# Recurrent branch's last part in 22 steps of one weight tile each, and more tiles between block transposes and their readers

## The chip, the cores and the metric

The kernel runs on one core of one Trainium2 chip. The metric is the device time of one execution in microseconds (us); the median of several runs is compared. The engines are TensorE (PE, matmuls; PEld is its weight load), VectorE (DVE), ScalarE (ACT), GpSimd (POOL) and SyncE (SP, which here only issues DMAs).

## The reference

One decoder layer on 256 tokens of width 2048, all in float32. `rmsnorm(x)` is multiplied by one wide matrix `w_in`, whose columns feed three branches and three merge gates:

- A: attention with 8 heads of 128 over a block of 256 tokens (there is only one block, so it is plain causal attention), times `silu(gate)`.
- B: attention with 16 query heads of 64, 4 key heads, a window of 128 and sinks, times `silu(gate)`.
- C: a convolution of 4 taps, then a gated linear recurrence, times `silu(gate)`:

```python
r = sigmoid(conv_block @ w_r + b_r);  i = sigmoid(conv_block @ w_i + b_i)
log_a = -8 * r * softplus(-lam);      a = exp(log_a)
b = sqrt(max(-expm1(2 * log_a), 0)) * (i * conv)
h[t] = a[t] * h[t-1] + b[t]
```

Each branch's output of width 1024 is projected to 2048, weighted by its sigmoid merge gate and summed; the sum goes through `w_out` and is added to x. A gated per-layer embedding and a last norm follow.

## The kernel before

**Weights.** Every weight matrix streams through in tiles of 128 x 1024 float32 (512 KB). `fetch` issues the load on SP into one of four raw buffers. `split` (lines 118, 119) makes two parts of it: ACT casts it to the high part `wh`, DVE subtracts and gives the low part `wl`; each has four buffers. `mm3` (lines 162 to 164) multiplies high by high, low by high, and high by low. A tile has 12 matmuls of 512 columns. A raw buffer is free again when DVE has made the low part.

**Order.** The tile framework's planner simulates the engines and writes each engine's order. Instructions come by their place in the program; `split` is moved ahead by a priority offset (LEAD), so casts and low parts run some three tiles ahead of PE. `issue_after(x)` ties an instruction behind `x` on the same engine. `tick()` is called once for each weight tile, right behind its `split`. It runs timers that are due (`later(SETTLE, ...)`) and takes one step from the list `todo`, all tied behind the newest cast on ACT and the newest low part on DVE. `hand_out` puts the steps of several generators into `todo`: a new one begins every `period` ticks (11 in branch A, 7 in B), and every step advances all that live.

**Exchange through DRAM.** `flip` (lines 582 to 587) turns a matrix: a block transpose on DVE, a DMA of the tile to DRAM, and four DMAs back, all issued on SP. Readers take `flipped` views. For a SiLU gate, `silu` flips the projected half and registers `gate` (lines 455, 456) SETTLE ticks later. For attention probabilities, `turned_probs` flips and then yields LATE times before `split_probs` (lines 611, 612) reads; `py`, the product with the values, follows. A pair of heads goes through these steps: bias (and, for each second pair of B, the group's key and value splits), scores (`q_b`, lines 688, 689), maximum (552 to 559), exponential (566), AHEAD ticks later norm (571 to 575) and flip, LATE ticks later `w_b` and `py`, and in the last step the final part (708 to 712 and the split of `zb`).

**Branch C.** `branch_c` is a generator. It projects and convolves, does the block products `pg`, and yields. The gate's SiLU and tanh, exponential and square over all 2048 columns come after the query projection of branch A, the bound, square root and the scaled inputs after the key projection, and the scans, the gated result and its split after the first gate half. These parts are not tied to ticks.

**Stages on the path.** In order: norm and value projections, branch C's and branch A's projections, merge of C (48 weight tiles, in which A's attention steps run), branch B's projections, merge of A (in which most of B's steps run), merge of B, `w_out`, and the embedding part.

Of the kernel before, what the change touches and what calls it, by code (L numbers as in the profile page):

```python
# [38 lines left out]
SLOT = 2112  # L39
QD = 32  # L40
AHEAD = 4
STEPS = 14
LATE = 5
TURN_LATE = 5
SETTLE = 8
RV = 384


# [1 line left out]
def trunk(ctx: ExitStack, tc: tile.TileContext, x, xt, p, table, onehot, maskv, w_in, sinks, conv, w_ri, vec, fin, w_br,  # L50
# [17 lines left out]
    def cols(k, n=1):  # L68
        return slice(k * SEQ, (k + n) * SEQ)
# [23 lines left out]
    los = []  # L93
    todo = []
    timers = []
    loads = []
    first_parts = {}

# [26 lines left out]
    def tick():  # L125
        due = []
        for t in timers:
            t[0] -= 1
            if t[0] == 0:
                due.append(t)  # L130
        timers[:] = [t for t in timers if t[0] > 0]
        if due or todo:
            with tc.issue_after(casts[-1]), tc.issue_after(los[-1]):
                for t in due:
                    t[1]()
                if todo:
                    todo.pop(0)()

    def drain():
        while todo:  # L140
            tick()
# [78 lines left out]
    def act_of(*units):  # L220
        return [tuple(t[:, cols(k)] for t in u) for u in units for k in range(KB)]

    def as_tiles(t):
        return t.rearrange("p (m a q) -> p m a q", a=4, q=QD)

    def split_act(u, k, n, src):
        hi, lo = (x[:, cols(k, n)] if len(src.shape) == 2 else as_tiles(x[:, cols(k, n)]) for x in u)
        ins = nc.scalar.copy(hi, src).ins
        nc.vector.tensor_tensor(lo, src, hi.bitcast(F32), op=ALU.subtract)
        return ins  # L230
# [209 lines left out]
    def chunk(t, c):  # L440
        return t[:, c * NH * CW : (c + 1) * NH * CW]

    def features(t, scale, name):
        for c in range(2):
            to_features(chunk(t, c), in_chunk(), scale, f"{name}{c}")
# [14 lines left out]
    def branch_c():  # L460
        xcT, cv, wri = block("xcT"), block("cv"), block("wri")
        rg, ig = block("rg"), block("ig")
        W1 = SEQ + CONV - 1
        xp = xcT[:, : KB * W1].rearrange("p (k t) -> p k t", k=KB)
        nc.vector.memset(xp[:, :, : CONV - 1], 0.0)
        cvk, rk, ik, hk = ktiles(cv), ktiles(rg), ktiles(ig), ktiles(xcT)
        wr = wri[:, : 2 * BW].rearrange("p (n d) -> p n d", n=KB)
        for c in range(2):
            t = temp(f"xc{c}").rearrange("p k t -> p (k t)")
            to_features(t, in_chunk(), rs1, f"xc{c}")  # L470

            def place(c=c, t=t):
                for h in range(NH):
                    to = xp[:, 4 * c : 4 * c + 4, CONV - 1 + h * P : CONV - 1 + (h + 1) * P]
                    nc.scalar.copy(to.rearrange("p j (a q) -> p j a q", a=4), flipped(t, 8)[:, h::NH])

            later(SETTLE, place)
        with tc.issue_after(casts[-1]):
            nc.scalar.dma_start(wri[:, : 2 * BW], w_ri)
        z = unit("zc")  # L480
        gs = [temp(f"gc{c}").rearrange("p k t -> p (k t)") for c in range(2)]
        for c in range(2):
            to_features(gs[c], in_chunk(), rs1, f"gc{c}")
        for k in range(KB):
            nc.vector.tensor_scalar(cvk[:, k, :], xp[:, k, 0:SEQ], convw[:, k : k + 1], conv_b[:, k : k + 1],
                                    op0=ALU.mult, op1=ALU.add)
            for j in range(1, CONV):
                nc.vector.scalar_tensor_tensor(cvk[:, k, :], xp[:, k, j : j + SEQ],
                                               convw[:, j * KB + k : j * KB + k + 1], cvk[:, k, :],
                                               op0=ALU.mult, op1=ALU.add)  # L490
            pg = aux(f"pg{k}")
            xs = split_small(cvk[:, k, :], f"cv{k}")
            ws = split_small(wr[:, k, :], f"wr{k}")
            for g in range(2):
                mm3(pg[:, g * SEQ : (g + 1) * SEQ], [t[:, g * P : (g + 1) * P] for t in ws], xs, True, True)
                nc.scalar.activation((rk, ik)[g][:, k, :], pg[:, g * SEQ : (g + 1) * SEQ], AF.Sigmoid,
                                     bias=(b_r, b_i)[g][:, k : k + 1])
            nc.vector.tensor_scalar_mul(rk[:, k, :], rk[:, k, :], sp8[:, k : k + 1])
            nc.vector.tensor_tensor(ik[:, k, :], ik[:, k, :], cvk[:, k, :], op=ALU.mult)
        yield  # L500
        for c in range(2):
            s = temp(f"sig_gc{c}").rearrange("p k t -> p (k t)")
            nc.scalar.activation(s, gs[c], AF.Sigmoid)
            nc.vector.tensor_tensor(gs[c], gs[c], s, op=ALU.mult)
        n = KB * SEQ
        t, a, sq, i = xcT[:, :n], rg[:, :n], cv[:, :n], ig[:, :n]
        nc.scalar.activation(t, a, AF.Tanh)
        nc.scalar.activation(a, a, AF.Exp, scale=-1.0)
        nc.scalar.activation(sq, a, AF.Square)
        yield  # L510
        nc.vector.scalar_tensor_tensor(sq, sq, 1.0, t, op0=ALU.add, op1=ALU.mult)
        nc.vector.tensor_scalar_max(sq, sq, 0.0)
        nc.scalar.activation(sq, sq, AF.Sqrt)
        for c in range(4):
            o = cols(2 * c, 2)
            nc.vector.tensor_tensor(i[:, o], i[:, o], sq[:, o], op=ALU.mult)
        yield
        for c in range(2):
            o = cols(4 * c, 4)
            for k in range(4 * c, 4 * c + 4):  # L520
                nc.vector.tensor_tensor_scan(hk[:, k, :], rk[:, k, :], ik[:, k, :], 0.0, op0=ALU.mult, op1=ALU.add)
            g = flipped(gs[c], 8)
            nc.vector.tensor_tensor(g, g, as_tiles(xcT[:, o]), op=ALU.mult)
            split_act(z, 4 * c, 4, g)
        yield z

    quad = [slice(i * QD, (i + 1) * QD) for i in range(P // QD)]

# [60 lines left out]
    def flipped(t, n):  # L589
        return t.rearrange("p (a m q) -> p m a q", a=4, m=n)  # L590
# [136 lines left out]
    for c in range(2):  # L727
        token_values(vh, (first_ps, second_ps)[c], c * CW)

    def branch_a(between):  # L730
        qT, kT, g = block("qa"), block("ka"), block("ga")
        features(qT, rs_q[DA], "qa")
        between()
        features(kT, rs1, "ka")
        between()
        silu(chunk(g, 0), "ga0")
        between()
        silu(chunk(g, 1), "ga1")
        va = [[vh[:, c, h * DA : (h + 1) * DA] for h in range(NA)] for c in range(NH)]
        return attention_heads(feature_tiles(qT), feature_tiles(kT), va, g)  # L740

    def branch_b():
        qT, kv, g = block("qb"), block("kvb"), block("gb")
        ps = in_chunk()
        kT = kv[:, : 2 * SEQ]
        vt = ktiles(kv)[:, 2:4, :]
        to_features(kT, ps[:, :, : 2 * P], rs1, "kb")
        token_values(vt, ps[:, :, 2 * P :], 0)
        features(qT, rs_q[DB], "qb")
        kb = [flipped(kT, 4)[:, NH * i : NH * (i + 1)] for i in range(2)]  # L750
        todo.extend([lambda: None] * 3)
        z = attention_pairs(feature_tiles(qT), kb, vt, g)
        for c in range(2):
            silu(chunk(g, c), f"gb{c}")
        return z
# [41 lines left out]
    def merge(z, bi, br):  # L797
        if bi == 0:
            merged.extend(wide(block(f"merged{h}")) for h in range(2))
        for n in range(4):  # L800
            sg = token_major(temp(f"sg_{br}{n}"))
            ps = in_chunk()
            for h in range(NH):
                nc.scalar.activation(sg[:, h, :], ps[:, h, :], AF.Sigmoid, scale=rs1[:, h : h + 1])
            if bi == 2 and n == 0:
                drain()
            py = project(act_of(z), w_br, (bi * 4 + n) * KB * CW // WT, f"br{br}{n}")
            dst = merged[n // 2][:, :, half_cols(n)]
            if bi == 0:
                nc.vector.tensor_tensor(dst, py, sg, op=ALU.mult)  # L810
                continue
            nc.vector.tensor_tensor(sg, py, sg, op=ALU.mult)
            (nc.vector if bi == 2 else nc.gpsimd).tensor_tensor(dst, dst, sg, op=ALU.add)
            if bi == 2:
                if n % 2 == 0:
                    mT.append(unit(f"m{n // 2}"))
                (turn_later if n < 3 else turn)(mT[n // 2], n, merged[n // 2], "m")

    steps = branch_c()
    next(steps)  # L820
    zcs = []
    za = branch_a(lambda: zcs.append(next(steps)))
    zc = zcs[-1]
    merge(zc, 0, "c")
    drain()
    zb = branch_b()
# [154 lines left out]
```

## Time and profile before

| | us |
|---|---|
| median of 3 runs | 1006.89 |
| lowest, highest | 1005.89, 1007.75 |
| the profiled execution | 1007.54 |
| its span | 1005.8 |
| PE busy in it | 984.7 (98%) |
| DVE busy | 658.2 (65%) |
| ACT busy | 555.5 (55%) |

The span is what the profiler's records cover; the execution's own time is 1.7 us longer. The shares are means over stages. The granted clock of TensorE was full (1.00, 2.4 GHz) in all slices between the first and the last.

### The profile page before, as it was taken

How to read it: one execution, taken by the hardware profiler on the slowest of the kernel's cores; microseconds unless marked ns; L12 is line 12 of the kernel's file. 1: busy time of each engine (PE TensorE's matmuls, PEld its weight loads, DVE VectorE, ACT ScalarE, POOL GpSimd, SP SyncE). 2: the span in 40 equal slices, each digit the busy share in tenths (PEclk: the TensorE clock that was granted, in tenths of full speed). 3: DMA queues.
4: the chain of work that ended last, by engine and by line, in shares of the span. 5: the costliest groups of instructions: out<-in, count | busy, mean ns of one | idle time of the engine just before them, and what ended most of it. 6: DMA issues, size and time to landing. Idle time of an engine off the chain costs nothing.

```text
span 1005.8 us, 12594 instructions
## 1 busy us (share of the span) xinstructions
PE 984.7 (98%) x4510; PEld 819.1 (81%) x4510; DVE 658.2 (65%) x950; ACT 555.5 (55%) x780; POOL 16.5 (2%) x14
## 2 busy tenths in 40 slices
PE   9999999999999999999999889999999999999996
PEld 7888888888788888888888768878888888888886
DVE  5765766665966567554577778796556655665764
ACT  7644446558565656544457557755444444554652
POOL 0000000000000000000000011011000000000000
PEclk9999999999999999999999999999999999999998
DMA  9867777665786665657777857677577776779652
GB/s 325 310 192 241 252 241 241 226 233 177 241 282 229 243 198 191 216 191 229 256 241 230 236 183 240 208 219 238 199 230 231 239 275 210 247 252 321 222 189 84
DMA packets 82774, 231.59 MB, mean 230 GB/s; under 512 B 9320, under 2 KB 30232, under 8 KB 82200
## 3 DMA queue, kind: packets, MB, share of 16 engines
q1 hardware_dynamic: 76176, 218.14, 66.5%
q10 hardware_dynamic: 6536, 12.65, 3.5%
q8 instruction: 35, 0.57, 0.2%
q14 instruction: 27, 0.22, 0.1%
HBM read 210.53 MB, written 20.22 MB: 229 GB/s over the span
## 4 chain that ended last, share of the span: by engine, by line
PE 80%; DVE 7%; DMA 5%; ACT 4%; issue 3%; SPq 1%; ACTq 0%; POOLq 0%; POOL 0%; DVEq 0%
PE ps_in L163 17%; PE ps_in L164 17%; PE ps_in L162 17%; PE ps_out L162 3%; PE ps_out L164 3%; PE ps_out L163 3%; PE ps_pg L162 3%; PE ps_pg L163 3%; PE ps_pg L164 3%; DVE wl_in L119 2%; PE ps_brc L162 1%; PE ps_brc L164 1%; PE ps_brb L164 1%; PE ps_brb L162 1%; PE ps_brc L163 1%
## 5 line engine op out<-in xcount | busy, mean ns | idle before, releaser
L119 DVE TENSOR_TENSOR wl_in<-r_in,wh_in 128x1024 fp32r<-128x1024 f32 x232 | 281.9, 1220 | 178.5 <-ACT wh_in L118 177.8
L163 PE MATMUL ps_in<-wl_in,h 128*128 128x512 f32 x928 | 361.8, 390 | 1.9 <-DVE wl_in L119 1.9
L162 PE MATMUL ps_in<-wh_in,h 128*128 128x512 f32 x928 | 361.8, 390 | 0.0
L164 PE MATMUL ps_in<-wh_in,h 128*128 128x512 f32 x928 | 361.3, 389 | 0.0
L118 ACT CAST wh_in<-r_in 128x1024 fp32r<-128x1024 f32 x232 | 242.2, 1052 | 208.5 <-PE ps_in L164 159.4
L163 PEld LDWEIGHTS ps_in<-wl_in,h 128*128 128x128 f32 x928 | 174.2, 188 | 38.7 <-DVE wl_in L119 3.5
L164 PEld LDWEIGHTS ps_in<-wh_in,h 128*128 128x128 f32 x928 | 174.3, 188 | 36.1
L162 PEld LDWEIGHTS ps_in<-wh_in,h 128*128 128x128 f32 x928 | 174.3, 188 | 35.5
L163 PE MATMUL ps_pg<-wl_pg,x_hi 128*128 128x512 f32 (+1 forms) x160 | 55.3, 347 | 0.0
L164 PE MATMUL ps_pg<-wh_pg,x_lo 128*128 128x512 f32 (+1 forms) x160 | 55.3, 347 | 0.0
L162 PE MATMUL ps_pg<-wh_pg,x_hi 128*128 128x512 f32 (+1 forms) x160 | 55.3, 347 | 0.0
L119 DVE TENSOR_TENSOR wl_out<-r_out,wh_out 128x1024 fp32r<-128x1024 f32 x32 | 38.8, 1223 | 24.9 <-ACT wh_out L118 24.9
L119 DVE TENSOR_TENSOR wl_pg<-r_pg,wh_pg 128x1024 fp32r<-128x1024 f32 x32 | 38.8, 1222 | 24.1 <-ACT wh_pg L118 24.0
L118 ACT CAST wh_out<-r_out 128x1024 fp32r<-128x1024 f32 x32 | 33.2, 1051 | 35.3 <-PE ps_out L164 29.0
L118 ACT CAST wh_pg<-r_pg 128x1024 fp32r<-128x1024 f32 x32 | 33.3, 1052 | 31.1 <-PE ps_pg L164 21.2
L162 PE MATMUL ps_out<-wh_out,m_hi 128*128 128x512 f32 x128 | 49.9, 390 | 0.0
L164 PE MATMUL ps_out<-wh_out,m_lo 128*128 128x512 f32 x128 | 49.8, 389 | 0.0
L163 PE MATMUL ps_out<-wl_out,m_hi 128*128 128x512 f32 x128 | 49.8, 389 | 0.0
L163 PEld LDWEIGHTS ps_pg<-wl_pg,x_hi 128*128 128x128 f32 x160 | 30.2, 189 | 3.8
L164 PEld LDWEIGHTS ps_pg<-wh_pg,x_lo 128*128 128x128 f32 x160 | 30.2, 189 | 3.8
L162 PEld LDWEIGHTS ps_pg<-wh_pg,x_hi 128*128 128x128 f32 x160 | 30.2, 189 | 3.7
L119 DVE TENSOR_TENSOR wl_brb<-r_brb,wh_brb 128x1024 fp32r<-128x1024 f32 x16 | 19.6, 1223 | 17.2 <-ACT wh_brb L118 17.2
(237 smaller groups left out, 1116.8 us busy)
## 6 DMA issues: line engine op xcount, KB each, us to landing
r_in<-w_in_dram SPq DMA_DIRECT2D x232, 512.0 KB, 4.1
r_out<-w_out_dram SPq DMA_DIRECT2D x32, 512.0 KB, 4.3
r_pg<-w_pg_dram SPq DMA_DIRECT2D x24, 512.0 KB, 5.4
r_brc<-w_br_dram SPq DMA_DIRECT2D x16, 512.0 KB, 3.7
r_bra<-w_br_dram SPq DMA_DIRECT2D x16, 512.0 KB, 3.9
r_brb<-w_br_dram SPq DMA_DIRECT2D x16, 512.0 KB, 4.7
r_pg<-w_pgt_dram SPq DMA_DIRECT2D x8, 512.0 KB, 3.3
d_b<-flip_b SPq DMA_DIRECT2D x8, 384.0 KB, 3.3
```

Source lines behind the costliest of these rows:

```text
L118: casts.append(nc.scalar.copy(hi[:, c], r[:, c]).ins)
L119: los.append(nc.vector.tensor_tensor(lo[:, c], r[:, c], hi[:, c].bitcast(F32), op=ALU.subtract).ins)
L162: nc.tensor.matmul(ps, ah, bh, start=first, stop=False)
L163: nc.tensor.matmul(ps, ah, bl, start=False, stop=False)
L164: nc.tensor.matmul(ps, al, bh, start=False, stop=last)
```

## The change

- Branch C no longer yields. It returns its unit `zc` and a list of 22 small steps (`rest`), each over half of the columns (or two scans). They go into a new list `side` behind the first half of the key projection, and `tick()` takes one step of `side` as well as one of `todo`. `merge` runs what is left of `side` before a branch's projection.
- `LATE` goes from 5 to 6 (and `STEPS` from 14 to 15), `SETTLE` from 8 to 10, and the empty steps ahead of branch B's pairs from 3 to 5.

```diff
-STEPS = 14
-LATE = 5
+STEPS = 15
+LATE = 6
 TURN_LATE = 5
-SETTLE = 8
+SETTLE = 10
...
-        if due or todo:
+        if due or side or todo:
             with tc.issue_after(casts[-1]), tc.issue_after(los[-1]):
                 for t in due:
                     t[1]()
-                if todo:
-                    todo.pop(0)()
+                for q in (side, todo):
+                    if q:
+                        q.pop(0)()
...
-        nc.scalar.activation(t, a, AF.Tanh)
-        nc.scalar.activation(a, a, AF.Exp, scale=-1.0)
-        nc.scalar.activation(sq, a, AF.Square)
-        yield
-        nc.vector.scalar_tensor_tensor(sq, sq, 1.0, t, op0=ALU.add, op1=ALU.mult)
-        nc.vector.tensor_scalar_max(sq, sq, 0.0)
-        nc.scalar.activation(sq, sq, AF.Sqrt)
...
+        def decays(c):
+            nc.scalar.activation(a[c], a[c], AF.Exp, scale=-1.0)
+
+        def bound(c):
+            nc.vector.scalar_tensor_tensor(sq[c], sq[c], 1.0, t[c], op0=ALU.add, op1=ALU.mult)
+            nc.vector.tensor_scalar_max(sq[c], sq[c], 0.0)
+
+        def inputs(c):
+            nc.vector.tensor_tensor(i[c], i[c], sq[c], op=ALU.mult)
+
+        def scan(k):
+            for m in range(k, k + 2):
+                nc.vector.tensor_tensor_scan(hk[:, m, :], rk[:, m, :], ik[:, m, :], 0.0, op0=ALU.mult, op1=ALU.add)
+
+        def result(c):
+            g = flipped(gs[c], 8)
+            nc.vector.tensor_tensor(g, g, as_tiles(t[c]), op=ALU.mult)
+
+        steps = [(gate, 0), (gate, 1)]
+        steps += [(lambda c: nc.scalar.activation(t[c], a[c], AF.Tanh), c) for c in range(2)]
+        steps += [(decays, c) for c in range(2)]
+        steps += [(lambda c: nc.scalar.activation(sq[c], a[c], AF.Square), c) for c in range(2)]
+        steps += [(bound, c) for c in range(2)]
+        steps += [(lambda c: nc.scalar.activation(sq[c], sq[c], AF.Sqrt), c) for c in range(2)]
+        steps += [(inputs, c) for c in range(2)]
         for c in range(2):
-            o = cols(4 * c, 4)
...
+            steps += [(scan, 4 * c), (scan, 4 * c + 2), (result, c)]
+            steps.append((lambda c: split_act(z, 4 * c, 4, flipped(gs[c], 8)), c))
+        return z, [lambda f=f, c=c: f(c) for f, c in steps]
...
         features(qT, rs_q[DA], "qa")
-        between()
-        features(kT, rs1, "ka")
-        between()
-        silu(chunk(g, 0), "ga0")
-        between()
-        silu(chunk(g, 1), "ga1")
+        for c in range(2):
+            to_features(chunk(kT, c), in_chunk(), rs1, f"ka{c}")
+            side.extend(rest)
+            rest = []
+        for c in range(2):
+            silu(chunk(g, c), f"ga{c}")
...
-        todo.extend([lambda: None] * 3)
+        todo.extend([lambda: None] * 5)
...
+            while side:
+                side.pop(0)()
             py = project(act_of(z), w_br, (bi * 4 + n) * KB * CW // WT, f"br{br}{n}")
...
-    steps = branch_c()
-    next(steps)
-    zcs = []
-    za = branch_a(lambda: zcs.append(next(steps)))
-    zc = zcs[-1]
+    zc, rest = branch_c()
+    za = branch_a(rest)
```

## Rows read from the trace of the kernel before

**Rows 1.** The page: its first line, and PE's and the other engines' busy time.

```profile
span 1005.8 us, 12594 instructions
...
PE 984.7 (98%) x4510; PEld 819.1 (81%) x4510; DVE 658.2 (65%) x950; ACT 555.5 (55%) x780; POOL 16.5 (2%) x14
```

**Rows 2.** Windows of 20 us: length, then busy us (and instructions) of PE, PEld, DVE, ACT and POOL, then the granted clock, the DMA share and GB/s.

```profile
260.00:280.00 20.00, 19.03 (x84) 15.46 (x83) 18.39 (x19) 10.21 (x11) 0.00 (x0) 1.00 0.60 201
...
560.00:580.00 20.00, 16.99 (x78) 13.63 (x76) 15.48 (x35) 11.60 (x18) 0.00 (x0) 1.00 0.76 244
580.00:600.00 20.00, 15.57 (x70) 12.33 (x70) 16.52 (x29) 12.82 (x25) 3.24 (x1) 1.00 0.49 163
600.00:620.00 20.00, 20.00 (x94) 16.66 (x93) 17.02 (x37) 13.94 (x25) 0.00 (x0) 1.00 0.73 231
620.00:640.00 20.00, 20.00 (x93) 16.68 (x92) 17.59 (x32) 13.09 (x26) 3.31 (x1) 1.00 0.69 230
640.00:660.00 20.00, 19.24 (x89) 15.89 (x88) 15.01 (x33) 12.99 (x25) 0.00 (x0) 1.00 0.65 214
660.00:680.00 20.00, 19.30 (x85) 15.40 (x84) 18.91 (x36) 13.03 (x23) 3.25 (x1) 1.00 0.74 223
```

**Rows 3.** PE's timeline, the rows between 15 and 980 us before which PE was idle: start, us, engine, line and form, then in brackets the idle time and what ended it.

```profile
263.60 0.50 PE L163 MATMUL ps_in<-wl_in,h 128*128 128x512 f32 x1 [0.97 <-DVE wl_in L119]
...
563.38 0.93 PE L536 MATMUL py_b<-w_b,v_b 128*128 128x512 f32 x4 [3.01 <-DVE w_b L612]
...
581.09 0.93 PE L536 MATMUL py_b<-w_b,v_b 128*128 128x512 f32 x4 [1.05 <-DVE w_b L612]
585.48 0.50 PE L163 MATMUL ps_in<-wl_in,h 128*128 128x512 f32 x1 [0.50 <-DVE wl_in L119]
592.85 0.47 PE L536 MATMUL s_b<-k_b,q_b 128*128 128x256 f32 x2 [1.86 <-DVE q_b L689]
594.34 0.72 PE L536 MATMUL s_b<-k_b,q_b 128*128 128x256 f32 x4 [1.02 <-DVE q_b L689]
...
656.85 0.70 PE L536 MATMUL s_b<-k_b,q_b 128*128 128x256 f32 x4 [0.76 <-DVE q_b L689]
666.38 0.50 PE L163 MATMUL ps_in<-wl_in,h 128*128 128x512 f32 x1 [0.39 <-DVE wl_in L119]
669.49 0.93 PE L536 MATMUL py_b<-w_b,v_b 128*128 128x512 f32 x4 [0.31 <-DVE w_b L612]
```

**Rows 4.** ACT's timeline in the recurrent branch's last part (columns as in rows 3).

```profile
238.47 1.28 ACT L508 ACT_TABLE_LOAD   x1
...
250.22 1.28 ACT L513 ACT_TABLE_LOAD   x1
251.98 1.93 ACT L513 ACTIVATE cv<-cv 128x2048 f32<-128x2048 f32 x1 [0.47 <-DVE cv L512]
...
261.25 1.05 ACT L118 CAST wh_in<-r_in 128x1024 fp32r<-128x1024 f32 x1 [3.20 <-DMA r_in<-w_in_dram]
```

**Rows 5.** DVE's timeline in the same stretch.

```profile
246.25 2.29 DVE L511 SCALAR_TENSOR_TENSOR cv<-cv,xcT 128x2048 f32<-128x2048 f32 x1 [0.59 <-ACT cv L509]
...
250.76 1.18 DVE L512 TENSOR_SCALAR cv<-cv 128x2048 f32<-128x2048 f32 x1
...
258.26 4.17 DVE L521 TENSOR_TENSOR_SCAN xcT<-rg,ig 128x256 f32<-128x256 f32 x7
262.35 1.20 DVE L119 TENSOR_TENSOR wl_in<-r_in,wh_in 128x1024 fp32r<-128x1024 f32 x1
```

**Rows 6.** ACT's timeline in branch B's steps: the gates of its two halves, the exponentials and the casts of the turned probabilities.

```profile
530.54 1.28 ACT L455 ACT_TABLE_LOAD   x1 [2.07 <-DMA gb<-d_gb]
...
553.63 0.20 ACT L563 ACTIVATE st2b<-st2b 128x4 f32<-128x4 f32 x1 [4.29 <-DVE st2b L558]
...
558.75 1.28 ACT L455 ACT_TABLE_LOAD   x1 [2.11 <-DMA gb<-d_gb]
560.05 1.06 ACT L455 ACTIVATE sig_gb<-gb 128x1024 f32<-128x1024 f32 x1
561.01 0.82 ACT L611 CAST w_b<-turn_b 128x768 fp32r<-128x768 f32 x1
...
579.12 0.83 ACT L611 CAST w_b<-turn_b 128x768 fp32r<-128x768 f32 x1 [5.83 <-DMA turn_b<-d_b]
...
603.42 0.83 ACT L611 CAST w_b<-turn_b 128x768 fp32r<-128x768 f32 x1 [3.55 <-DMA turn_b<-d_b]
```

**Rows 7.** The waits between 500 and 690 us: who waited for whom, us in total, times, longest.

```profile
ACT w_b L611 <- DMA turn_b<-d_b: 21.5, 6, 5.8
```

**Rows 8.** DVE's timeline in branch B's steps (norm, query split, final part, block transpose, and the head group's key split).

```profile
565.69 1.00 DVE L575 TENSOR_SCALAR e_b<-e_b,st1b 128x256 f32<-128x256 f32 x4
566.73 0.87 DVE L689 TENSOR_TENSOR q_b<-qb,q_b 64x256 fp32r<-64x256 f32 x2
...
568.77 0.85 DVE L710 TENSOR_TENSOR qb<-py_b,qb 64x256 f32<-64x256 f32 x2
569.65 0.98 DVE L582 STREAM_TRANSPOSE flip_b<-e_b 128x768 f32<-128x768 f32 x1
570.55 0.38 DVE L712 TENSOR_TENSOR gb<-qb,gb 128x256 f32<-128x256 f32 x1
...
589.89 0.84 DVE L671 TENSOR_TENSOR k_b<-kvb,k_b 64x256 fp32r<-64x256 f32 x2
```

More of the change, by code (lines that the diff above doesn't have):

```diff
@@ L95, in trunk @@
     timers = []
+    side = []
     loads = []
@@ L499, in branch_c, with gate @@
             nc.vector.tensor_tensor(ik[:, k, :], ik[:, k, :], cvk[:, k, :], op=ALU.mult)
-        yield
-        for c in range(2):
+        n = KB * SEQ // 2
+        t, a, sq, i = ([b[:, c * n : (c + 1) * n] for c in range(2)] for b in (xcT, rg, cv, ig))
+        def gate(c):
             s = temp(f"sig_gc{c}").rearrange("p k t -> p (k t)")
@@ L504, in branch_c @@
             nc.vector.tensor_tensor(gs[c], gs[c], s, op=ALU.mult)
-        n = KB * SEQ
-        t, a, sq, i = xcT[:, :n], rg[:, :n], cv[:, :n], ig[:, :n]
-        nc.scalar.activation(t, a, AF.Tanh)
-        nc.scalar.activation(a, a, AF.Exp, scale=-1.0)
-        nc.scalar.activation(sq, a, AF.Square)
-        yield
-        nc.vector.scalar_tensor_tensor(sq, sq, 1.0, t, op0=ALU.add, op1=ALU.mult)
-        nc.vector.tensor_scalar_max(sq, sq, 0.0)
-        nc.scalar.activation(sq, sq, AF.Sqrt)
@@ L514, in branch_c @@
[L514 to L517, printed above, removed]
-        for c in range(2):
-            o = cols(4 * c, 4)
[L520 to L524, printed above, removed]
@@ L525, in branch_c @@
-        yield z
+        def decays(c):
[8 more added lines that the diff above has]
+                nc.vector.tensor_tensor_scan(hk[:, m, :], rk[:, m, :], ik[:, m, :], 0.0, op0=ALU.mult, op1=ALU.add)
@@ L728, in trunk, with branch_a @@
         token_values(vh, (first_ps, second_ps)[c], c * CW)
-    def branch_a(between):
+    def branch_a(rest):
         qT, kT, g = block("qa"), block("ka"), block("ga")
         features(qT, rs_q[DA], "qa")
-        between()
-        features(kT, rs1, "ka")
-        between()
-        silu(chunk(g, 0), "ga0")
-        between()
-        silu(chunk(g, 1), "ga1")
+        for c in range(2):
[4 more added lines that the diff above has]
+            silu(chunk(g, c), f"ga{c}")
         va = [[vh[:, c, h * DA : (h + 1) * DA] for h in range(NA)] for c in range(NH)]
```

## The prediction

> **What bounds the kernel now.** The page comes first. The span is 1005.8 us and PE is busy for 984.7 us of it [rows 1]. So the most that an edit of the order can win is PE's idle time, 21.1 us, and only the part of it that lies inside the span, since the change touches neither the start nor the tail. The second view is the windows [rows 2]: PE is full (20.00 of 20 us) everywhere between 20 and 980 us but in five windows. It misses 0.97 us in 260 to 280, 3.01 and 4.43 us in 560 to 600, and 0.76 and 0.70 us in 640 to 680: 9.87 us in all. The third view, PE's timeline, gives the nine gaps one by one with what ended each [rows 3]; 0.97 + (3.01 + 1.05 + 0.50 + 1.86 + 1.02) + (0.76 + 0.39 + 0.31) is the same 9.87 us. Every one was ended by DVE: a low part of a weight tile (line 119), a low part of turned probabilities (line 612), or a query split (line 689). A full PE runs at 19.03 us for 84 matmuls [rows 2], 0.227 us each, so one weight tile (12 matmuls) takes 2.7 us. That is the clock of this kernel: one tick of the planner's steps is 2.7 us.
>
> The last views, ACT's and DVE's timelines around those gaps, show what made DVE late. At 263 us it is the recurrent branch: DVE runs a 2.29 us instruction over all 2048 columns, and later seven scans for 4.17 us; the low part of a tile comes only behind them, and a tile's cast on ACT waits 3.20 us for its load, whose raw buffer had been freed late [rows 4, 5]. At 560 us it is the gate of branch B. ACT first waits 4.29 us for a row maximum of DVE, then 2.07 and 2.11 us (the second at 558.75) for the exchanged gate, then loads a table (1.28 us) and does the sigmoid (1.06 us); only then comes the cast of the turned probabilities at 561.01, and PE, whose product was placed for an earlier time, stands until 563.38 [rows 3, 6]. From there on DVE is late, so the next block transpose starts at 569.65, while ACT reaches the reader of its exchange at 573.3 and waits 5.83 us, until 579.12 [rows 6, 8]. The four gaps up to 594 follow from that wait. Later pairs repeat it in small: six waits for that exchange sum to 21.5 us [rows 7].
>
> **The change, part by part.** The number of matmuls and weight loads does not change; only order and waiting time do, so each term is a part of the 9.87 us.
>
> The recurrent branch. Before, whole-width instructions stand in the queues wherever the planner found room. After, 22 steps come one per tick, and each is tied behind that tick's cast and low part. The 2048-column instructions become two of 1024. On ACT a half costs 1.06 us (the sigmoid of that width) against 1.93 for the whole [rows 4, 6], so four functions cost 4 x (2.12 - 1.93) = 0.8 us more. On DVE a half costs about 1.20 us (a 1024-column low part) against 2.29 for the whole [rows 5]: 0.1 us more. The heaviest tick on DVE (the method `bound`) has 1.20 us and half of 1.18, with an overhead 0.65, beside a low part of 1.20: 3.05 us in 2.7, twice [rows 5]; two scans are 4.17 x 2 / 7 = 1.2 us. Three buffers of weights ahead of PE hide 0.35 us twice. The 3.20 us wait goes because no low part stands behind more than 1.9 us of DVE work. The term is -0.97 us; the bounds are -0.97 and 0.
>
> Table loads of ACT. The last part has three, of 1.28 us each: before the exponential, back to the sigmoid for the last gate block, and before the square root; the first and the last are shown [rows 4]. With half steps the sigmoids of the last two blocks can fall between tanh, exponential and square root, so I count up to three more, 3.8 us of ACT. I take 0 for PE: the window there has ACT at 10.21 of 20 us [rows 2], and the cast is tied ahead of each step.
> The Trainium skill (ScalarE: Activation LUTs, section on table sets) says to batch calls by table set, all of one set and then all of the next; cutting a chain into steps speaks against that. Taken wholly on PE's path it would give 3.8 us back, 1002.6 us by the sum below. No row before shows such steps, so the trace neither confirms nor refutes it.
>
> SETTLE from 8 to 10. The gate of a SiLU half and the placing of the convolution's input come two ticks later, 5.4 us. The gate's waits for the exchange, 2.07 and 2.11 us [rows 6], are smaller than that and go. Covered readers: the first final that uses the gate comes two ticks behind it.
>
> LATE from 5 to 6, STEPS 14 to 15. ACT sat idle before the cast of the turned probabilities and waited for the exchange alone [rows 6], so what moves is its place in the queue: one tile, 2.7 us, later. The waits of 5.83 and 3.55 us [rows 6] shrink to at most 3.1 and 0.9, and the whole 21.5 us [rows 7] to about 21.5 - 6 x 2.7 = 5. Nothing else moves earlier. The final of a pair moves one tick with it. Two more empty ticks stand ahead of branch B's steps, so its pairs and the gate's transposes drift apart by two ticks. All steps still fit: branch A's 4 x 11 + 4 = 48 into the 48 tiles of the first merge, branch B's 5 + 56 + 8 = 69 into 72 tiles, the recurrent 22 into 24.
>
> So the cluster of 7.44 us between 560 and 597: the 3.01 us gap loses the exchange wait, but gate and turned probabilities of the second pair now fall in one tick, and the table load of 1.28 us may still stand ahead of the cast; I leave 1.3 us. The 4.43 us that follow from the 5.83 us wait go, since the wait does. Term: -6.1 us (bounds -7.44 and -2). The 1.46 us of the later pairs: half a query wait may stay, 0.5; term -1.0 us (bounds -1.46 and 0). New waits: I allow nothing, bounds 0 and +2.
>
> Sum: -0.97 - 6.1 - 1.0 = -8.1 us. The profiled execution took 1007.5 us, 1.7 us more than its span, and the median of the runs is 1006.9; the span would be 997.7 us, and the median 1006.9 - 8.1 = **998.8 us**. No gap at all would be 997.0 us.
>
> **Rivals.** *First: DVE is the limit in branch B, not the exchange.* DVE's busy time in the six windows from 560 to 680 is 15.48 + 16.52 + 17.02 + 17.59 + 15.01 + 18.91 = 100.5 us [rows 2]. Without the gaps the same work must fit in 120 - 8.9 = 111.1 us, 90%. In the two of these windows in which PE stayed full DVE was busy for 17.3 of 20 us. If it cannot be kept busier than that, 100.5 / 0.865 = 116.2 us are needed, 5.1 us of gaps stay, and the time is 997.0 + 5.1 = 1002.1 us. For it: all gaps were ended by DVE. Against it: 18.91 of 20 in the last window, at a gap of only 0.70.
>
> *Second: the gate still holds the turned probabilities.* If the planner puts gate, table load and cast in the old order and PE's product at its old distance, the cluster stays, and only 0.97 and some of the 1.46 us go: 1005 us. Against it: two extra tiles exceed the measured waits.
>
> *Third, slower: a burst on DVE in every pair.* Pairs start every 7 ticks, and with 15 steps the final of one pair shares its tick with norm and transpose of the next and the head work of the one after. From the rows: final 0.85 + 0.38 and about 0.4 for its low part, norm 1.00 and about 0.3 of small ones, transpose 0.98, head 0.84 + 0.3 every second pair, low part 1.2 [rows 8]: 6.3 us in 2.7, and 2.1 in the next tick for the query split (0.87) that PE waits on. Over two ticks 8.4 us stand against 5.4: 3.0 us, 1.9 without head work. If DVE has no lead, 4 x 3.0 + 4 x 1.9 = 19.6 us of new gaps, less the 8 us won: 1018 us. It decides as soon as DVE leads PE by less than about one tile. Against it: in the old trace the final already follows norm and query split directly on DVE [rows 8], so the pile is not new.
>
> *Fourth: nothing.* If DVE's order is set by data and the constants move nothing, 1006.9 us.
>
> **How the numbers follow.** Likeliest, 998.8, its own range 997 to 1001.5: 0.68. First rival: 0.14. Second: 0.08, half of it above 1004.9 us. Third: 0.06. Fourth: 0.04. Two runs of this kernel can be told apart from about 0.2%, 2 us. So faster by more than that is 0.68 + 0.14 + 0.04 = 0.86, within it 0.04 + 0.04 = 0.08, slower 0.06. The range takes in the first two cases and leaves out the last three, 0.18: 996.6 to 1003.8 us.
>
> **What would show it.** Right: no PE gap between 245 and 290 us, and scans in pairs with low parts between them; ACT's waits for the exchanged probabilities about 5 us in total instead of 21.5, and none on the gate; PE's gaps between 540 and 680 us at most 3 us in sum. The first rival shows as gaps ended by DVE while ACT does not wait on DMA; the second as a cast of turned probabilities behind a table load, with PE waiting; the third as query-split waits in every pair. I am wrong if a new gap appears in branch A, whose steps also move, or if the table loads delay casts beyond three tiles.

## The result, and the profile after

| kernel | median us | before, same runs | ratio, 95% interval |
|---|---|---|---|
| changed | 1001.33 (999.84 to 1002.71) | 1006.89 | 0.9936 [0.9922, 0.9951] |
| changed, second set of runs | 1000.31 (999.84 to 1001.89) | 1006.15 | 0.9944 [0.9931, 0.9958] |

The change makes the kernel faster by 0.6%: 5.6 and 5.8 us. Forecast were 8.1 us and 998.8 us, with a range of 996.6 to 1003.8. All times in this document are of executions in the chip's faster state; one execution of the experiment with `LATE` 5 took 2022.92 us and is left out. In the changed kernel the lines have moved: cast 119, low part 120, `split_probs` 624 and 625, query split 701 and 702, block transpose 595, the exchange's DMAs 597 (to DRAM) and 600 (back), weight loads 104.

The page, first line and busy times:

```profile
span 999.3 us, 12592 instructions
...
PE 984.9 (99%) x4510; PEld 818.9 (82%) x4510; DVE 659.8 (66%) x950; ACT 560.2 (56%) x786; POOL 13.9 (1%) x14
```

PE's busy time is the same to 0.2 us, so the 6.5 us by which the span is shorter are idle time. PE's timeline, all rows between 15 and 980 us ahead of which PE was idle (this answers to [rows 3]):

```profile
237.86 0.50 PE L165 MATMUL ps_in<-wl_in,h 128*128 128x512 f32 x1 [0.20 <-DVE wl_in L120]
...
572.62 1.16 PE L549 MATMUL s_b<-k_b,q_b 128*128 128x256 f32 x6 [1.51 <-DVE q_b L702]
...
584.02 0.50 PE L165 MATMUL ps_in<-wl_in,h 128*128 128x512 f32 x1 [0.72 <-DVE wl_in L120]
...
608.19 0.96 PE L549 MATMUL py_b<-w_b,v_b 128*128 128x512 f32 x4 [0.21 <-DVE w_b L625]
...
620.60 0.50 PE L165 MATMUL ps_in<-wl_in,h 128*128 128x512 f32 x1 [0.24 <-DVE wl_in L120]
629.23 0.93 PE L549 MATMUL py_b<-w_b,v_b 128*128 128x512 f32 x4 [0.41 <-DVE w_b L625]
...
656.62 1.17 PE L549 MATMUL s_b<-k_b,q_b 128*128 128x256 f32 x6 [0.50 <-DVE q_b L702]
```

The sum is 3.79 us where it was 9.87. In the recurrent branch 0.97 became 0.20; in 560 to 600 us 7.44 became 2.23; after 600 us 1.46 became 1.36. The waits of ACT on DMA between 500 and 690 us (us in total, times, longest; the first answers to [rows 7]):

```profile
ACT w_b L624 <- DMA turn_b<-d_b: 3.6, 2, 2.6
...
ACT wh_in L119 <- DMA r_in<-w_in_dram: 4.8, 2, 2.6
ACT wh_bra L119 <- DMA r_bra<-w_br_dram: 4.8, 3, 2.9
```

The wait for the turned probabilities fell by 17.9 us, from 21.5 to 3.6, more than the 16.5 us of the forecast, and no wait for the gate is left. Yet the gaps after 600 us are as large in sum as before, mostly at other instructions. And a wait has come that was 0.4 us before: 9.6 us for weight tiles.

### The profile page after: what moved, and what is told of

Same layout as the page of the kernel before. It is cut to its first block, busy times and chain, and to the rows that moved or that the text cites. A ratio compares the mean times of both kernels' runs of the same rounds, so it can differ in the third digit from the quotient of the medians.

```text
span 999.3 us, 12592 instructions
## 1 busy us (share of the span) xinstructions
PE 984.9 (99%) x4510; PEld 818.9 (82%) x4510; DVE 659.8 (66%) x950; ACT 560.2 (56%) x786; POOL 13.9 (1%) x14
## 4 chain that ended last, share of the span: by engine, by line
PE 85%; DVE 4%; ACT 4%; DMA 3%; issue 3%; SPq 0%; POOLq 0%; ACTq 0%; POOL 0%; DVEq 0%
PE ps_in L165 18%; PE ps_in L166 18%; PE ps_in L164 18%; PE ps_out L166 3%; PE ps_out L164 3%; PE ps_out L165 3%; PE ps_pg L164 3%; PE ps_pg L165 3%; PE ps_pg L166 3%; DVE wl_in L120 2%; PE ps_brc L164 1%; PE ps_brc L166 1%; PE ps_brb L166 1%; PE ps_brb L165 1%; PE ps_brc L165 1%
## 5 line engine op out<-in xcount | busy, mean ns | idle before, releaser
L120 DVE TENSOR_TENSOR wl_in<-r_in,wh_in 128x1024 fp32r<-128x1024 f32 x232 | 287.4, 1239 | 173.0 <-ACT wh_in L119 172.4
L120 DVE TENSOR_TENSOR wl_brc<-r_brc,wh_brc 128x1024 fp32r<-128x1024 f32 x16 | 19.6, 1222 | 19.2 <-ACT wh_brc L119 19.2
```

The lines of the kernel that those rows point to most:

```text
L120: los.append(nc.vector.tensor_tensor(lo[:, c], r[:, c], hi[:, c].bitcast(F32), op=ALU.subtract).ins)
```

## The experiments

Each was timed beside the kernel before, on the same chip, in three sets; so ratios are compared, and medians only within a set.

### The two parts alone

The steps alone: the changed kernel with the old constants.

```diff
-STEPS = 15
-LATE = 6
-SETTLE = 10
+STEPS = 14
+LATE = 5
+SETTLE = 8
...
-        todo.extend([lambda: None] * 5)
+        todo.extend([lambda: None] * 3)
```

> The 22 steps of the recurrent branch alone: LATE 5, STEPS 14, SETTLE 8 and three empty steps, as before the change. Theory (waits for the exchange make branch B's gaps): the 0.97 us gap near 263 us falls to 0.3 us or less, the nine-gap cluster of branch B stays near 9 us, time about 1006 us, ratio to the kernel before about 0.999. Rival (the steps shift everything behind them, and branch B's gain comes from that): a good part of the 6 us, about 1003 us or less.

Measured: 1006.06 us against 1007.98, ratio 0.9978 [0.9970, 0.9987]. PE has no gap between 220 and 300 us. All gaps sum to 6.79 us, those between 540 and 680 us to 6.59. The two of 1.05 and 0.50 us are missing, the large one stays.

```profile
561.89 0.93 PE L549 MATMUL py_b<-w_b,v_b 128*128 128x512 f32 x4 [2.64 <-DVE w_b L625]
590.54 0.47 PE L549 MATMUL s_b<-k_b,q_b 128*128 128x256 f32 x2 [1.51 <-DVE q_b L702]
```

But idle time is not all that branch B lost here. Right behind the gap of 2.64 us TensorE's granted clock fell. A window of 1 us (columns as in [rows 2]) and two of PE's rows:

```profile
564.00:565.00 1.00, 1.00 (x3) 0.73 (x3) 1.00 (x5) 0.94 (x4) 0.00 (x0) 0.50 0.87 279
563.74 0.63 PE L165 MATMUL ps_in<-wl_in,h 128*128 128x512 f32 x1
564.17 0.63 PE L166 MATMUL ps_in<-wh_in,h 128*128 128x512 f32 x1
```

The clock is 0.50 (1.2 GHz) there and 1.00 (2.4 GHz) again from 567 us. Eight matmuls start 0.43 us apart instead of 0.227, which costs 1.6 us while PE counts as busy. Idle and slow time together are 8.2 us, near the 9 us of the theory; that the slow matmuls gave DVE the time in which the two small gaps closed is likely, not shown. In the profile before, the gap of 3.01 us was followed by a full clock. Of the 18 executions of the kernel before in this set, 15 have a mean clock of 0.993 to 0.996 and three of 0.997 or 0.998; all ten of the changed kernel have 0.997 or 0.998. That fits such a fall in most executions of the kernel before, though a mean cannot show where the clock fell. The times of the three lie among those of the 15.

The constants alone: the kernel before with LATE 6, STEPS 15, SETTLE 10 and five empty steps.

> The four constants alone (LATE 6, STEPS 15, SETTLE 10, five empty steps) on the kernel before, whose recurrent part keeps its whole-width instructions. Theory: a gap of about 1 us near 263 us stays, branch B's gaps are those of the changed kernel (3.6 us instead of 8.9), time about 1002 us. Rival: branch B's gaps stay above 6 us, and the time is 1004 us or more.

Measured: 1000.53 us, ratio 0.9932 [0.9918, 0.9946], the same as the whole change. The gaps sum to 2.47 us, and the recurrent branch's is 0.34, not 1:

```profile
254.62 0.50 PE L163 MATMUL ps_in<-wl_in,h 128*128 128x512 f32 x1 [0.34 <-DVE wl_in L119]
```

So the constants carry the gain. The 22 steps win some 2 us on the old constants and nothing that can be measured on the new ones, where the gap was 0.34 us without the steps and is 0.20 with them.

### Undoing one constant

`LATE` 5 and `STEPS` 14 again:

```diff
-STEPS = 15
-LATE = 6
+STEPS = 14
+LATE = 5
```

> The changed kernel with LATE 5 and STEPS 14 again. Theory (exchange of the probabilities): ACT's waits for the turned probabilities rise from 3.6 us to 12 us or more, and PE's gaps between 540 and 680 us from 3.6 to about 6, time about 1003.5 us. Rival (DVE's load is the limit in branch B): waits of ACT rise, PE's gaps stay within 1 us of 3.6, time 1001 to 1002 us.

Measured: 1004.60 us, ratio 0.9969 [0.9959, 0.9980]. ACT's waits for the turned probabilities are 18.9 us again, and PE's gaps between 540 and 680 us 5.38 us:

```profile
ACT w_b L624 <- DMA turn_b<-d_b: 18.9, 8, 4.1
```

`SETTLE` 8 again (`-SETTLE = 10`, `+SETTLE = 8`):

> The changed kernel with SETTLE 8 again. Theory: ACT waits for the gate's exchange again, about 2 us for each half, and a gap of some 2 to 3 us stands before the second pair's product near 560 us, time about 1004 us. Rival: the two empty steps and LATE have already drawn gate and pairs apart, and the gate's wait falls into slack: 1001 to 1002 us.

Measured: 1002.27 us, ratio 0.9948 [0.9935, 0.9960]. ACT waits 5.3 us for the gate, and the product of the second pair waits as in [rows 3]:

```profile
565.40 0.98 PE L549 MATMUL py_b<-w_b,v_b 128*128 128x512 f32 x4 [2.56 <-DVE w_b L625]
```

Yet the time lies between theory and rival, and its interval overlaps those of the changed kernel, so with five empty steps no effect of `SETTLE` on the time is shown. In this profile too the clock is at 0.50 behind the large gap, between 567 and 570 us. The waits that come back are those that the forecast named for both constants.

### What the rest is: a repeat, the additions on POOL, the empty steps, one tile more

The changed kernel again, unedited, for scale:

> The changed kernel itself, unedited, beside the next three on the same chip. Both theories: about 1001 to 1002 us, gaps of 3 to 4 us between 540 and 680 us; how far its single gaps differ from the first profile tells what a difference of one gap means.

Measured: 1000.31 us, ratio as in the table above. All gaps between 540 and 680 us come again at the same instructions, six of six; five of them agree within 0.04 us. Only the first differs: 0.22 us against 1.51, behind ACT's waits for `r_bra`, 3.2 us against 4.8. So the order is fixed and the DMA's landing varies. The sum is 2.25 us.

The sum of branch A's merge on DVE:

```diff
-            (nc.vector if bi == 2 else nc.gpsimd).tensor_tensor(dst, dst, sg, op=ALU.add)
+            nc.vector.tensor_tensor(dst, dst, sg, op=ALU.add)
```

> The changed kernel with the sum of branch A's merge on DVE instead of POOL (four additions of 128 x 1024). Theory (each addition on POOL blocks DVE for about 2.1 us, and three of the six remaining gaps, 0.72, 0.24 and 0.50 us, follow from it): DVE's 3.2 us instructions go, these gaps go, time 1 to 1.5 us below the changed kernel. Rival (DVE's load is the limit, and four more instructions of 1.2 us make it worse): gaps grow, time 1 us or more above it.

Measured: 997.30 us, ratio 0.9910 [0.9897, 0.9924], 3.0 us below the changed kernel in the same set. The gaps fall from 2.45 us to 0.51. What the addition does to DVE is seen in the changed kernel: POOL's timeline, and the DVE instruction in whose time it falls.

```profile
580.49 2.39 POOL L828 TENSOR_TENSOR merged<-merged,sg_a 128x1024 f32<-128x1024 f32 x1 [523.88 <-DVE sg_a L827]
617.00 2.45 POOL L828 TENSOR_TENSOR merged<-merged,sg_a 128x1024 f32<-128x1024 f32 x1 [34.13 <-DVE sg_a L827]
651.96 2.40 POOL L828 TENSOR_TENSOR merged<-merged,sg_a 128x1024 f32<-128x1024 f32 x1 [32.50 <-DVE sg_a L827]
```

```profile
580.67 3.29 DVE L120 TENSOR_TENSOR wl_in<-r_in,wh_in 128x1024 fp32r<-128x1024 f32 x1
...
617.11 3.43 DVE L120 TENSOR_TENSOR wl_in<-r_in,wh_in 128x1024 fp32r<-128x1024 f32 x1
...
651.74 3.16 DVE L588 TENSOR_SCALAR e_b<-e_b,st1b 128x256 f32<-128x256 f32 x4
```

A low part takes 3.29 and 3.43 us instead of 1.2 [rows 5], and four norms 3.16 instead of 1.0 [rows 8]: DVE stands for 2.1 to 2.2 us. Right behind follow PE's gaps at 584.02, 620.60 and 656.62. On DVE the addition itself costs 1.22 us. The two gaps between them, 608.19 and 629.23, went as well; the one that is left, 0.32 us, is the first. The Trainium skill (SBUF — State Buffer, section on its two separate sides) says that GpSimd and VectorE share one pair of ports as an exclusive lock, held for a whole instruction; the low part's extra time, 2.1 us beside the addition's 2.39, agrees.

Three empty steps instead of five:

```diff
-        todo.extend([lambda: None] * 5)
+        todo.extend([lambda: None] * 3)
```

> The changed kernel with three empty steps ahead of branch B's pairs instead of five. Theory (the two ticks draw the gate's transpose and the pairs' transposes apart): gate and turned probabilities wait on the exchange together again, PE's gaps between 540 and 680 us rise by 1 to 2 us, time about 1003 us. Rival (the two ticks do nothing): within 0.7 us of the changed kernel.

Measured: 996.60 us, ratio 0.9904 [0.9890, 0.9917], **3.7 us below the changed kernel**: both theory and rival fall. Branch B has no gap; between 15 and 980 us only the 0.19 us of the recurrent branch is left. SP's timeline tells what the two steps do. In the changed kernel:

```profile
541.07 0.33 SPq L597 DMA_DIRECT2D d_gb<-flip_gb  x1
547.41 1.75 SPq L600 DMA_DIRECT2D gb<-d_gb  x4
549.25 0.38 SPq L104 DMA_DIRECT2D r_bra<-w_br_dram  x1
549.73 0.38 SPq L597 DMA_DIRECT2D d_b<-flip_b  x1
550.20 1.16 SPq L104 DMA_DIRECT2D r_bra<-w_br_dram  x2
555.40 2.47 SPq L600 DMA_DIRECT2D turn_b<-d_b  x4
557.97 0.38 SPq L104 DMA_DIRECT2D r_bra<-w_br_dram  x1
```

With three empty steps:

```profile
541.38 0.33 SPq L597 DMA_DIRECT2D d_gb<-flip_gb  x1
542.24 0.33 SPq L597 DMA_DIRECT2D d_b<-flip_b  x1
545.70 1.74 SPq L600 DMA_DIRECT2D gb<-d_gb  x4
547.54 1.80 SPq L600 DMA_DIRECT2D turn_b<-d_b  x4
549.44 3.20 SPq L104 DMA_DIRECT2D r_bra<-w_br_dram  x4
```

SP's waits for the writes to DRAM (us in total, times, longest), first with five empty steps, two rows, then with three:

```profile
SPq L600 <- DMA d_gb<-flip_gb: 6.0, 1, 6.0
SPq L600 <- DMA d_b<-flip_b: 4.0, 1, 4.0
...
SPq L600 <- DMA d_gb<-flip_gb: 3.1, 1, 3.1
```

In these rows SP issues its DMAs one behind the other, and the DMAs back wait until the write to DRAM has landed. With three empty steps the gate's and the pair's exchange go together, and SP stands once for them, from 542.6 to 545.7 us. With five they are drawn apart: SP stands from 541.4 to 547.4 and again from 551.4 to 555.4, with weight loads queued behind both. The last `r_bra` of the four goes out at 557.97 instead of before 552.64. ACT then waits for weights and once, 2.6 us, for the turned probabilities. That DVE, busy for 14.5 to 18.8 us of each 20 from 560 to 660 us, then does not get its lead back is argued from this. The stands alone do not make the cost: with the additions on DVE, above, SP's order was that of five empty steps, and the ratio was 0.9910 against 0.9904 here, with overlapping intervals.

One tile more, LATE 7 and STEPS 16:

```diff
-STEPS = 15
-LATE = 6
+STEPS = 16
+LATE = 7
```

> The changed kernel with LATE 7 and STEPS 16. Theory (with LATE 6 the exchange is covered, and what is left is DVE's and POOL's): ACT's wait for the turned probabilities goes from 3.6 us to under 1, PE's gaps stay within 1 us, time 1000.5 to 1002 us. Rival (the exchange still costs): gaps fall by 2 us or more, time 999 us.

Measured: 998.71 us, ratio 0.9924 [0.9912, 0.9937], 1.6 us below the changed kernel, though the intervals overlap. The time is the rival's; the gaps fell from 2.25 to 1.34 us, less than the rival's 2. ACT no longer waits for the probabilities, but one gap of 1.34 us stands at 654.56, behind POOL's third addition. The empty steps stayed five here, so it also moves when exchange and loads meet; what of the gain is the wait's was not separated.

### What the two empty steps cost, and what the smallest version is

The gate's exchanges in branch B issued on POOL's queue, five empty steps kept:

```diff
-        nc.sync.dma_start(d, t)
+        queue = nc.gpsimd if name.startswith("gb") else nc.sync
+        queue.dma_start(d, t)
...
-            nc.sync.dma_start(dst[quad[b]].rearrange("i (a c) -> i a c", a=4), back[b])
+            queue.dma_start(dst[quad[b]].rearrange("i (a c) -> i a c", a=4), back[b])
```

> The changed kernel (five empty steps), the DMAs of the gate's two exchanges in branch B (gb0, gb1) issued on POOL's queue instead of SP's; the order on PE, DVE and ACT is the same. Theory (with five empty steps the gate's and the pair's exchange no longer go together, SP's queue stands twice for a write to DRAM, the weight loads behind it come late by some 4 us, and DVE and ACT run without lead from there): ACT's waits for r_bra near 555 us (4.8 us in the first profile) fall under 1.5, most of the gaps go, time 997 to 999 us. Rival (the two ticks put the pairs into a bad phase with the merge's work on DVE and POOL): the loads come early, the gaps after 580 us stay near 2 us, time within 1 us of the changed kernel's 1000.3.

Measured: 998.98 us, ratio 0.9930 [0.9917, 0.9942], about 1.4 us below the changed kernel's 0.9944, with overlapping intervals. The order on PE, DVE and ACT is unchanged; lines behind the edit are one further down. No wait for `r_bra` is left among ACT's waits on DMA, and the gaps at 572 and 584 us are gone. The four after 600 us are not:

```profile
605.87 0.97 PE L549 MATMUL py_b<-w_b,v_b 128*128 128x512 f32 x4 [0.15 <-DVE w_b L626]
618.27 0.50 PE L165 MATMUL ps_in<-wl_in,h 128*128 128x512 f32 x1 [0.22 <-DVE wl_in L120]
626.91 0.93 PE L549 MATMUL py_b<-w_b,v_b 128*128 128x512 f32 x4 [0.41 <-DVE w_b L626]
654.30 1.17 PE L549 MATMUL s_b<-k_b,q_b 128*128 128x256 f32 x6 [0.49 <-DVE q_b L703]
```

So theory and rival each hold for a part: without the gate's exchange on SP the first two gaps go, and the four later ones do not hang on it.

The kernel before with LATE 6, STEPS 15 and SETTLE 10 alone, three empty steps and no small steps:

> The kernel before with LATE 6, STEPS 15 and SETTLE 10, its three empty steps and its whole-width recurrent part. Theory (the longer distances alone win branch B; the 22 steps are worth their one gap of 0.3 to 1 us): 997 us, within 1 us of the kernel with steps and three empty steps (996.6). Rival (the steps are needed for it): 999 us or more.

Measured: 996.93 us, ratio 0.9911 [0.9897, 0.9926]; one gap of 0.34 us. Three constants give all that can be measured, 2.5 to 3.3 us more than the whole change (0.9936 and 0.9944).

Three empty steps and SETTLE 8 (`-SETTLE = 10`, `+SETTLE = 8` on the version with three):

> The changed kernel with three empty steps and SETTLE 8: the 22 steps and LATE 6 are what is left of the change. Theory (the gate's reader must come later too, or ACT waits about 2 us for it ahead of the second pair's turned probabilities): a gap of 1 to 3 us near 560 us returns, time 998 to 1000 us. Rival (LATE covers it all): 996.6 us, no gap.

Measured: 999.59 us, ratio 0.9939 [0.9925, 0.9952]. The gap of the second pair is back, and its train:

```profile
562.24 0.93 PE L549 MATMUL py_b<-w_b,v_b 128*128 128x512 f32 x4 [1.17 <-DVE w_b L625]
...
588.52 0.70 PE L549 MATMUL s_b<-k_b,q_b 128*128 128x256 f32 x4 [1.02 <-DVE q_b L702]
```

SETTLE is worth 0.9939 against 0.9904, about 3.5 us, when the exchanges lie together. From the steps alone, above, this version differs by `LATE` and `STEPS` only: 0.9939 against 0.9978, about 3.9 us. The gaps between 540 and 680 us fall with it from 6.59 to 2.73 us, and those after 600 us from 1.42 to 0.39.

Three empty steps and the addition on DVE:

> The changed kernel with three empty steps and the sum of branch A's merge on DVE. Theory (POOL's hold on DVE costs only where DVE has no lead, and with three empty steps no gap is left): 996 to 997 us, as with three empty steps alone. Rival (fewer DVE stops still help, or four more DVE instructions hurt): a difference of 1 us or more either way.

Measured: 995.72 us, ratio 0.9898 [0.9884, 0.9912], the fastest version that was run. Against three empty steps alone (0.9904) the intervals overlap: the 3.0 us that the addition gave on the changed kernel are not there to be had a second time. POOL's hold is in the version with three empty steps too, and makes no gap there:

```profile
576.24 3.43 DVE L120 TENSOR_TENSOR wl_in<-r_in,wh_in 128x1024 fp32r<-128x1024 f32 x1 [0.21 <-ACT wh_in L119]
```

It costs where DVE has no lead, and nothing that can be measured where it has.

## Why the prediction was right in its range, and where it was off

**Bound and path: right in the main.** All gaps but two in one experiment (1.56 and 1.03 us with `LATE` 5, ended by a small DVE instruction of the softmax) were ended by the DVE results that the prediction named, and most of the gain is gaps that went. PE's idle time was not the whole account: a gap costs more than it shows (below), and behind a large one the clock can fall.

**The recurrent branch, -0.97: the gap went to 0.20, but not by the steps alone.** With the new constants alone it is 0.34. The wait for weights that I had expected the steps to remove is still there in size (between 220 and 300 us four waits of ACT for `r_in`, the longest 3.5 us); it just no longer reaches PE. Of the table loads I had counted up to three more. There are two more, five instead of three; four of them stand between 224 and 235 us, and ACT is busy for 19.54 of 20 us there:

```profile
220.00:240.00 20.00, 19.80 (x90) 16.13 (x89) 10.14 (x10) 19.54 (x21) 0.00 (x0) 1.00 0.54 175
```

The only gap left in this branch, 0.20 us, lies in that window. I had taken ACT's load from the window 260 to 280; the loads fell into another. Against the rule that the prediction took from the Trainium skill (ScalarE: Activation LUTs, section on table sets), to do all of one set and then all of the next, the change cost two more loads. The trace agrees with the rule by 2.6 us of ACT, and at most 0.2 us of PE.

**LATE: mechanism right, and larger than worked out** for the wait (21.5 to 3.6 us), worth 2.5 to 3.3 us of time with five empty steps and 3.9 with three. **SETTLE: mechanism right**, 3.5 us with three empty steps.

**The cluster, -6.1: it measured -5.2 in the first profile and -6.5 in the second.** This term was sized well, but what stayed was not the table load ahead of the cast. It was late weights, and at the second of the two gaps POOL's hold on DVE as well: it went with either of the two repairs. The sign set for a right forecast, at most 3 us of gaps between 540 and 680 us, failed in the first profile (3.59) and held in the second (2.25).

**The later pairs, -1.0: wrong for the change as it was made.** 1.46 became 1.36 and 1.35 us. I had read these gaps as the exchange's in small, because ACT waited 3 to 4 us ahead of each. With three empty steps that reading holds: a larger `LATE` takes them from 1.42 to 0.39 us, and `SETTLE` 10 takes the rest. So the gaps in their place are the two empty steps'. Three of the six between 540 and 680 us follow a hold of POOL's addition on DVE. That hold was in the trace of before, too, on instructions of 128 x 4 that take 0.15 us elsewhere:

```profile
587.61 2.36 DVE L571 TENSOR_TENSOR st1b<-st1b,st2b 128x4 f32<-128x4 f32 x1
...
622.66 2.35 DVE L558 TENSOR_TENSOR st2b<-sinkb,st0b 128x4 f32<-128x4 f32 x1
```

The first rival (DVE is the limit) had the right engine, and its sign was seen: gaps ended by DVE while ACT hardly waits on an exchange. But its sum was wrong. With three empty steps PE stays full from 540 to 680 us with DVE busy for 18.59 of 20 us in one window, above the 17.3 that I had taken for its ceiling.

**The two empty steps: the step that failed.** I put them down as a help (pairs and gate "drift apart") and gave "new waits" no value, with a bound of +2. They cost 3.7 us, with the additions on POOL as they are; with the additions on DVE it is some 1.2 us (0.9910 against 0.9898, intervals overlapping). I had followed the two exchanges to their readers and not to the queue that issues them. An exchange holds SP from its write to its landing, and every weight load behind it; two apart hold it twice. Without the two steps the change measured -9.6 us where I had forecast -8.1. So the total came into the range partly by luck: a gain that was 1.5 us larger than worked out, and a cost of 3.7 us that had been put at nothing.

**The floor of 997.0 leaves out what a gap costs beyond its idle time.** The medians do not contradict it: three empty steps, with 0.19 us of gaps, are at 0.9904 of the kernel before, 997.2 us on the forecast's scale. But in the profiles the span fell from 998.0 us in the repeat to 994.0 with three empty steps, while the gaps fell by 2.26 us; PE's busy time fell by the other part, from 984.9 to 983.0 us. One gap of the repeat shows how:

```profile
581.69 0.39 PE L164 MATMUL ps_in<-wh_in,h 128*128 128x512 f32 x1
582.76 0.50 PE L165 MATMUL ps_in<-wl_in,h 128*128 128x512 f32 x1 [0.68 <-DVE wl_in L120]
583.10 0.40 PE L166 MATMUL ps_in<-wh_in,h 128*128 128x512 f32 x1
```

A matmul's record lasts 0.39 us, but the next one starts 0.227 us after it when PE is full. Here the next starts 1.07 us after it, so 0.84 us are lost where 0.68 show; and the one behind comes after 0.34 us, another 0.11. The six gaps that went cost about 0.3 us each in this way, which is what was missing.

**What stays open.** Why the four gaps after 600 us go with three empty steps, when moving the gate's exchange off SP leaves them. They go as well when the additions move to DVE, so they need POOL's hold; but with three empty steps the holds are there and the gaps are not. The pairs then stand two tiles elsewhere against the merge's products and additions, and which of these meetings matters was not isolated.

## What to carry to other kernels

- A wait seen ahead of a cast is not yet the cause of the gap behind it. Take the wait away by a larger distance, and nothing else with it, and see whether the gap goes. Here small gaps seemed to stay because the same change brought new ones; the distance alone removed most of them.
- When two exchanges through DRAM share an in-order queue with loads, see whether they can be drawn together: follow a moved step to its queue and count for how long that stands.
- If PE runs gapless but for a few places, one engine's lost lead is what links them; several repairs of it, here 3.0 and 3.7 us alone, are then not worth their sum together (about 4.6 us by the ratios).

## What the runs showed of the hardware that was not expected

- An addition of 128 x 1024 on POOL stops DVE for 2.1 to 2.2 us, nearly as long as POOL takes (2.4 us); done on DVE it takes 1.22 us. Whichever DVE instruction came next stood, even one of 128 x 4 (2.36 us instead of 0.15).
- A DMA of 512 KB to DRAM held up its readers' issue on SP for 6.0 and 5.1 us in the two profiles of the changed kernel, and for 3.1 us, behind one more write, with three empty steps.
- Behind a gap of 2.64 us TensorE's granted clock fell to 0.50 for some 3 us, at a cost of 1.6 us that no idle time shows. It did the same behind one of 2.56 us, and did not behind one of 3.01.
- The span fell by more than PE's visible gaps did, by some 0.3 us for each of six gaps that went: part of a stall lies under the record of the matmul ahead of it, and the matmul behind it comes late too.
